# Two hybrid decoder layers on one core: attention's probabilities are turned by DMA in place of TensorE

## The chip, the core and the metric

The kernel runs on one core of a Trainium2 chip. A core has TensorE (PE; the profile lists its matrix multiplications as PE and its weight loads as PEld), VectorE (DVE), ScalarE (ACT), GpSimd (POOL) and SyncE (SP), whose queue here issues nearly all DMA transfers. The metric is the device time of one execution in microseconds, and a kernel's time is the median over its runs.

## What is computed

The reference is a trunk of two decoder layers over 256 tokens of width 1024, in float32. Each layer has a gated feed-forward network (FFN) of width 2816 added at half weight, a mixer, and a second FFN like the first:

```
for l in range(DEPTH):
    h = h + 0.5 * rmsnorm(swiglu(rmsnorm(h), ff1...))
    h = h + rmsnorm(hybrid_mixer(rmsnorm(h), ...))
    h = h + 0.5 * rmsnorm(swiglu(rmsnorm(h), ff2...))
```

The mixer projects its input and works on it with three groups side by side: a state space scan of 8 heads with a short convolution ahead of it, a pooling group, and causal attention with 4 heads of 64. For 256 tokens the attention's block choice is empty, so it is plain causal attention: `softmax(q k^T / 8)` times `v`. The three results are laid side by side and multiplied by an output matrix.

## The kernel before

Tokens lie in two tiles of 128 (t = 0, 1). Every float32 product with a weight is made of three matmuls of a shorter type: weights and inputs are split into a rounded part `hi` and a rest `lo`, and `hi*hi`, `hi*lo`, `lo*hi` are added up in PSUM.

The weights come in units of 1 MB. The class `Weights` plans them in the order of their use. `load` (line 75) issues a unit's transfer on SP into one of 4 raw buffers; `split_next` (line 95) makes `hi` on ScalarE (line 111) and `lo` on VectorE (line 112) into one of 5 pairs of buffers; `done` gives a pair back when the last matmul of the unit is in the program. `pump` (line 123) loads and splits as far as buffers allow. It loads only while `W.allowed`, a budget of loads, is above 0; `load` takes one off. If `W.behind` is set, the next load is ordered behind that transfer on SP's queue. The program text gives priorities: a scheduler lays out each engine's fixed order, taking the first instruction in the text that its model says is ready. `tc.issue_after(x)` orders instructions on one engine behind x, and `tc.keep_in_program_order` pins matmuls.

In the FFN some tiles are turned by DMA. `send` (line 482) takes a tile of 128 x 512 float32, lets ScalarE part it into its upper and lower 16-bit halves (line 485, 128 x 1024 of type uint16) and has SP issue a transposing transfer (line 489), eight blocks of 128 x 128 halves. `receive` (line 494) joins the turned halves to float32 again on ScalarE (line 497).

The mixer of one layer goes, in the order of the text: projections to q, k, v (`first`, line 712); the tap products of the convolution (`taps`, matmuls on line 327) for B, C, x0, x1; `qT`, `kT` and the scores into PSUM (line 840); `softmax` (line 843) for the first 128 queries over 128 keys (p0) and for the other 128 over 256 keys (p1), two tiles each, one for each of j = 0, 1, that hold two heads: the exponentials on ScalarE (line 854), the scaling on VectorE (line 858). Then come the segments of the scan (lines 770 and 772), three silus (line 795) and the products of B and C (lines 886 to 891). Behind these the probabilities are turned: eight transposes on PE (lines 898, 899) and four (line 905), from PSUM to `pT0` and `pT1` by three copies on ScalarE (lines 901, 908). Then taps x1, the product u for pooling (line 923, copied on line 926), the first half of z (`zed(0)`, matmuls on line 367), attention (`attend`, lines 972 and 974, which reads `pT0`, `pT1` and v), the transposes of x (line 998), the second half of z, pooling (line 1057), the scan (line 1019), its gating (lines 1027 to 1031) and turning (line 1037), and the output product (line 389, pinned). Attention and the transposes of x are ordered behind z's first half, and z's second half behind the transposes of x:

```
        sz0 = zed(0)
        d = pool_means()
        with tc.issue_after(zed.last.ins):
            y_attn = attend()
            turn_x(0)
            turn_x(1)
        with tc.issue_after(turn_x.last.ins):
            sz1 = zed(1)
```

Of the kernel before, what the change touches and what calls it, by code (L numbers as in the profile page):

```python
# [13 lines left out]
U16 = mybir.dt.uint16  # L14
AF = mybir.ActivationFunctionType
# [3 lines left out]
P = 128  # L19
# [128 lines left out]
def hybrid_trunk_kernel(ctx: ExitStack, tc: tile.TileContext, a, out: bass.AP):  # L148
    nc = tc.nc
# [9 lines left out]
    def buf(dtype=F32, n=512, tag="t"):  # L159
        return tmp.tile([P, n], dtype, tag=tag, name=f"{tag}{next(ids)}", bufs={"t": 20, "n": 8}[tag])  # L160

    def tiny(n):
        return small.tile([P, n], F32, tag=f"s{n}", name=f"s{next(ids)}", bufs=2 if n > 64 else 12)

    def bank(tag="wk"):
        return psum.tile([P, 512], F32, tag=tag, name=f"{tag}{next(ids)}")

    def banks2():
        return [bank("acc"), bank("acc")]

    W = Weights(tc, rawp, splitp)

    h = consts.tile([P, NT, D], F32, name="h")
# [6 lines left out]
    ident = consts.tile([P, P], F32, name="ident")  # L180
# [274 lines left out]
    def ffn_first(t, p, pin=False, ahead=None, between=None, by_dma=False):  # L455

        ps = [bank(), bank()]
        for i in range(2):
            mm_half(ps[i], [p["f", i, k] for k in range(2)], t, pin, ahead if i else None)
            if not i:  # L460
                s = buf()
                nc.scalar.activation(s, ps[0], AF.Silu)
        hf = gate(*ps, s)
        with tc.issue_after(pre_turn.lower.ins):
            if between:
                W.split_next()
                between()

            W.pump(SPLIT_BUFS - t)
        return send(hf) if by_dma else hf  # L470
# [8 lines left out]
                    nc.tensor.transpose(ps[:, j * S + t * P : j * S + (t + 1) * P], hf[t][:, c], ident)  # L479
            split_into(hT[i], (slice(None), slice(None)), ps)  # L480

    def send(x):

        halves = buf(U16, 1024)
        part = nc.scalar.activation(halves.rearrange("p (a n) -> p a n", a=2),
                                    x[:, :].bitcast(U16).rearrange("p (n a) -> p a n", a=2), AF.Copy)
        turned = buf(U16, 1024)
        with tc.issue_after(part.ins):
            t = nc.sync.dma_start_transpose(turned.rearrange("p (a n) -> p a n", a=8), halves)
        if W.allowed < 10:  # L490
            W.allowed, W.behind = 10**6, t.ins
        return turned

# [44 lines left out]
    def ffn_quad(i, p, left, turn, downs, by_dma):  # L538
# [41 lines left out]
        def second():  # L580
            product(pd, left["X22"], p["T4", i], False)
            nc.scalar.activation(w2, pd, AF.Silu)
            nc.vector.tensor_tensor(h1, h1, w2, op=ALU.mult)
            hf[1] = send(h1) if by_dma else h1
            W.pump()
# [121 lines left out]
    def mixer(l, p, turned, next_left, before_next):  # L707
# [42 lines left out]
        z, z2, q = tiny(16), tiny(16), tiny(16)  # L750
# [42 lines left out]
        def act(name, acc):  # L793
            conv[name] = buf()
            return nc.scalar.activation(conv[name], acc, AF.Silu)
# [6 lines left out]
        for w in range(2):  # L802
            ps = bank("acc")
# [4 lines left out]
            c = buf()  # L808
# [27 lines left out]
        for n, ps in ((P, s0), (2 * P, s1)):  # L836
            for pr in range(2):
                for j in range(2):
                    r = slice(j * 64, (j + 1) * 64)
# [2 lines left out]

        def softmax(ps, n):

            pr_ = [buf(n=2 * n) for _ in range(2)]
            mx, sm = tiny(4), tiny(4)
            for j in range(2):
                nc.vector.tensor_reduce(mx[:, 2 * j : 2 * j + 2], ps[j][:, : 2 * n].rearrange("p (a n) -> p a n", a=2),
                                        axis=AX.X, op=ALU.max)
            nc.vector.tensor_scalar(mx, mx, -0.125, None, op0=ALU.mult)  # L850
            for j in range(2):
                for a in range(2):
                    s, i = slice(a * n, (a + 1) * n), slice(2 * j + a, 2 * j + a + 1)
                    nc.scalar.activation(pr_[j][:, s], ps[j][:, s], AF.Exp, scale=0.125, bias=mx[:, i], accum_out=sm[:, i])
            nc.vector.reciprocal(sm, sm)
            for j in range(2):
                x = pr_[j].rearrange("p (a n) -> p a n", a=2)
                nc.vector.tensor_tensor(x, x, sm[:, 2 * j : 2 * j + 2, None].to_broadcast([P, 2, n]), op=ALU.mult)
            return pr_

        p0 = softmax(s0, P)
        p1 = softmax(s1, 2 * P)


        ps = bank()
# [10 lines left out]
        act("B", accB)  # L876
        act("C", accC)
        act("x0", accx)
        W.pump()


        cbs = []
        for g in range(2):
            B_, C_ = conv["B"][:, g * 256 : (g + 1) * 256], conv["C"][:, g * 256 : (g + 1) * 256]
            ps = bank("acc")
            nc.tensor.matmul(ps[:, : 2 * P], B_[:, :P], C_, start=True, stop=True)
            nc.tensor.matmul(ps[:, 2 * P : 3 * P], B_[:, P:], C_[:, P:], start=True, stop=True)
            c = buf(n=384).rearrange("p (b n) -> p b n", b=3)
            ps = ps[:, :384].rearrange("p (b n) -> p b n", b=3)
# [1 line left out]
            nc.scalar.activation(c[:, 1, :], ps[:, 1, :], AF.Copy)  # L891
            cbs.append(c)

        pT0 = [None, None]
        for j in range(2):
            ps = bank("acc")
            for pr in range(2):
                nc.tensor.transpose(ps[:, pr * 256 : pr * 256 + P], p0[j][:, pr * P : (pr + 1) * P], ident)
                nc.tensor.transpose(ps[:, pr * 256 + P : (pr + 1) * 256], p1[j][:, pr * 256 : pr * 256 + P], ident)
            pT0[j] = buf()  # L900
            nc.scalar.activation(pT0[j], ps, AF.Copy)
        ps = bank("acc")
        for j in range(2):
            for pr in range(2):
                nc.tensor.transpose(ps[:, (2 * j + pr) * P : (2 * j + pr + 1) * P],
                                    p1[j][:, pr * 256 + P : (pr + 1) * 256], ident)
        pT1 = buf()
        nc.scalar.activation(pT1, ps, AF.Copy)

        for c in range(2):  # L910
            for g in range(2):
# [12 lines left out]
        W.done(p["u"])  # L924
        u = buf()
        nc.scalar.activation(u, pu, AF.Copy)
        W.pump()

        def pool_means():
# [135 lines left out]
        acc = [banks2(), banks2()]  # L1065
# [68 lines left out]
    for l in range(DEPTH):  # L1134
        def step(n):

            def f(t):
                r = pre_scale(t)
                if t == 1:
                    load_gain(1, l + n // 3, 2 * (n % 3) + 1)  # L1140
                    if 3 * l + n + 1 < 3 * DEPTH:
                        load_gain(0, l + (n + 1) // 3, 2 * ((n + 1) % 3))
                return r
            return f

        def store(t, s):
            q = nc.scalar if t == NT - 1 and s.start else nc.sync
            q.dma_start(out[t * P : (t + 1) * P, s], h[:, t, s])

        f1, mx, f2 = plans[l]  # L1150
        end = l == DEPTH - 1
        turned = ffn(l, 1, f1, FFN_GAIN, turned, left, None, step(1), False, None if l else later)
        left = {}
        turned = mixer(l, mx, turned, left, step(2))
        left, now = None if end else {}, left
        turned = ffn(l, 2, f2, FFN_GAIN, turned, now, left, store if end else step(3), end)
# [98 lines left out]
```

## Time and profile before

| what | value |
|---|---|
| median of 3 runs | 924.17 us (924.09 to 925.56) |
| the profiled execution | 923.65 us |
| its span, first to last instruction | 922.0 us |
| granted TensorE clock, mean | 0.997 |
| ScalarE busy | 627.0 us (68%) |
| the mixer's stage in layer 0, 205 to 281 us | PE busy 76.00 of 76 us, VectorE 63.87, ScalarE 50.60 |

The profile is of one execution. Busy times are sums over an engine's instructions; a matmul's length is drawn as if it stood alone, so that neighbours overlap. A row of the timeline gives start, length, engine, line, operation, what it writes and reads, how many instructions are merged in it, and in brackets how long the engine was idle ahead of it and which instruction ended that. The two layers are alike in the mixer: layer 1 runs 449.8 us behind layer 0 at these lines.

### The profile page before, as it was taken

Reading aid. Unit: us, or ns where it says so; the run is one execution under the profiler, and the core shown is the slowest. Engines: PE = TensorE matmul, PEld = TensorE weight load, DVE = VectorE, ACT = ScalarE, POOL = GpSimd, SP = SyncE. Lnnn points to the kernel's source line nnn. Section 1 sums busy time; section 2 is a strip of 40 time slices with the busy share of each in tenths; the row PEclk is TensorE's granted clock in tenths of the full one; section 3 lists DMA queues with packets and bytes.
Section 4 is the critical chain, followed back from the end, with each engine's and each line's share of the span. In section 5 each row is a group of like instructions: output and inputs, shape, how many; then the busy total and the mean of one; then the engine's idle time right before and its main releaser. Section 6 shows DMA issues by size and latency. Waiting matters only on the chain.

```text
span 922.0 us, 12352 instructions
## 1 busy us (share of the span) xinstructions
PE 909.3 (99%) x4626; PEld 769.0 (83%) x4626; DVE 800.9 (87%) x1067; ACT 627.0 (68%) x1003; POOL 30.2 (3%) x49
## 2 busy tenths in 40 slices
PE   8999999999999999999999999999999999999997
PEld 5888887889988888888888888888998888888885
DVE  6999889689877999899599989987989699989972
ACT  7666657478747677667675866766795566867761
POOL 0000000000001000000000000000000110000000
PEclk9999999999999999999999999999999999999999
DMA  8576957556434577768655958593834145959641
GB/s 335 158 267 199 365 180 287 216 192 220 147 136 147 149 257 214 281 183 334 179 183 149 351 163 295 173 334 139 296 111 157 73 171 165 347 145 324 190 142 46
DMA packets 40671, 193.64 MB, mean 210 GB/s; under 512 B 15778, under 2 KB 16034, under 8 KB 18596
## 3 DMA queue, kind: packets, MB, share of 16 engines
q1 hardware_dynamic: 38740, 180.01, 54.2%
q0 software_dynamic: 1728, 12.58, 7.3%
q8 instruction: 36, 0.59, 0.2%
q10 hardware_dynamic: 144, 0.26, 0.1%
q14 instruction: 23, 0.19, 0.1%
HBM read 188.65 MB, written 1.05 MB: 206 GB/s over the span
## 4 chain that ended last, share of the span: by engine, by line
PE 95%; DVE 2%; issue 2%; ACT 1%; DVEq 0%; POOLq 0%; POOL 0%
PE acc L389 30%; PE wk L534 23%; PE wk L367 14%; PE wk L336 10%; PE wk L327 6%; PE wk L338 5%; DVE lo L112 1%; PE wk L354 1%; PE wk L278 1%; PE wk L1019 1%; PE wk L508 1%; PE acc L770 0%; PE acc L1102 0%; PE wk L479 0%; PE acc L840 0%
## 5 line engine op out<-in xcount | busy, mean ns | idle before, releaser
L112 DVE TENSOR_TENSOR lo<-raw,hi 128x1024 fp32r<-128x1024 f32 (+2 forms) x452 | 464.7, 1076 | 20.9 <-ACT hi L111 18.5
L111 ACT ACTIVATE hi<-raw 128x1024 fp32r<-128x1024 f32 (+2 forms) x452 | 399.8, 937 | 118.8 <-DMA raw<-in_ff_d 32.7
L389 PE MATMUL acc<-hi,t 128*128 128x512 f32 x832 | 215.9, 391 | 0.3 <-ACT t L227 0.3
L389 PEld LDWEIGHTS acc<-hi,t 128*128 128x128 f32 x832 | 154.6, 188 | 32.2 <-ACT t L227 1.2
L389 PE MATMUL acc<-lo,t 128*128 128x512 f32 x416 | 114.2, 390 | 0.0
L534 PE MATMUL wk<-hi,n 128*128 128x512 f32 x384 | 100.7, 390 | 0.8 <-DVE wk L560 0.8
L367 PE MATMUL wk<-hi,xT 128*128 128x512 f32 x384 | 99.6, 397 | 1.6 <-ACT hi L111 1.6
L336 PE MATMUL wk<-xT,hi 128*128 128x512 f32 x384 | 97.4, 394 | 0.0
L110 DVE TENSOR_TENSOR raw<-raw,raw 128x1024 f32<-128x1024 f32 x72 | 86.2, 1217 | 10.4 <-DMA raw<-in_ff_q 10.4
L389 PEld LDWEIGHTS acc<-lo,t 128*128 128x128 f32 x416 | 77.7, 188 | 16.0
L367 PEld LDWEIGHTS wk<-hi,xT 128*128 128x128 f32 x384 | 72.0, 191 | 16.9 <-ACT hi L111 1.9
L534 PEld LDWEIGHTS wk<-hi,n 128*128 128x128 f32 x384 | 71.7, 188 | 15.8 <-ACT hi L111 1.2
L336 PEld LDWEIGHTS wk<-xT,hi 128*128 128x128 f32 x384 | 69.9, 188 | 13.3
L534 PE MATMUL wk<-hi,xT 128*128 128x512 f32 x288 | 77.3, 390 | 0.9 <-DVE t L567 0.8
L534 PEld LDWEIGHTS wk<-hi,xT 128*128 128x128 f32 x288 | 53.7, 188 | 13.2 <-ACT hi L111 1.2
L338 PEld LDWEIGHTS wk<-xT,lo 128*128 128x128 f32 x384 | 52.3, 190 | 3.8
L338 PE MATMUL wk<-xT,lo 128*128 128x256 f32 x384 | 53.5, 282 | 0.0
L367 PE MATMUL wk<-lo,xT 128*128 128x512 f32 x192 | 51.5, 390 | 0.0
L534 PE MATMUL wk<-lo,n 128*128 128x512 f32 x192 | 51.3, 389 | 0.0
L327 PE MATMUL wk<-xT,hi 128*128 128x256 f32 x320 | 42.5, 283 | 0.0
L367 PEld LDWEIGHTS wk<-lo,xT 128*128 128x128 f32 x192 | 36.0, 188 | 7.7
L534 PEld LDWEIGHTS wk<-lo,n 128*128 128x128 f32 x192 | 36.0, 188 | 7.5
(186 smaller groups left out, 890.0 us busy)
## 6 DMA issues: line engine op xcount, KB each, us to landing
raw<-in_ff_q SPq DMA_DIRECT2D x48, 1024.0 KB, 6.6
raw<-in_ff_d SPq DMA_DIRECT2D x44, 1024.0 KB, 6.0
raw<-in_ff_f SPq DMA_DIRECT2D x16, 1024.0 KB, 5.5
raw<-in_ff_q POOLq DMA_DIRECT2D x12, 1024.0 KB, 7.9
raw<-in_ff_g SPq DMA_DIRECT2D x12, 1024.0 KB, 4.8
raw<-in_ff_u SPq DMA_DIRECT2D x12, 1024.0 KB, 5.2
raw<-in_w_in SPq DMA_DIRECT2D x10, 1024.0 KB, 4.8
raw<-in_w_kvz SPq DMA_DIRECT2D x8, 1024.0 KB, 6.4
```

The source lines that it names most:

```text
L110: nc.vector.tensor_tensor(raw[:, s], self.raw[x][:, s], self.raw[y][:, s], op=op)
L111: self.act = nc.scalar.activation(hi[:, s], raw[:, s], AF.Copy)
L112: nc.vector.tensor_tensor(lo[:, s], raw[:, s], hi[:, s].bitcast(F32), op=ALU.subtract)
L278: pre_turn.last = nc.tensor.transpose(ps[:, k * P : (k + 1) * P], xn[i][:, k * P : (k + 1) * P], ident)
L327: nc.tensor.matmul(ps, w[:, k, s], y[:, k, :], start=i == 0 and k == 0, stop=i == 2 and k == KD - 1)
L336: nc.tensor.matmul(ps, hi[:, k, s], both[:, :, k, :], start=k == 0, stop=k == KD - 1)
L338: nc.tensor.matmul(ps[:, S:], lo[:, k, s], xT[0][:, k, :], start=False, stop=k == KD - 1, skip_group_check=True)
L354: nc.tensor.matmul(ps, x[:, k, s], w[:, k, :], start=i == 0 and k == 0, stop=i == 2 and k == KD - 1)
L367: m = nc.tensor.matmul(ps, y[:, k, :], w[:, k, :], start=h == 0 and n == 0, stop=h == 1 and n == len(parts) - 1)
L389: m = nc.tensor.matmul(acc[b], x[:, j, s], w[:, j, b * 512 : (b + 1) * 512], start=first and j == 0 and i == 0, stop=last and j == 1 and i ...
L508: nc.tensor.transpose(ps[:, c], x[:, c], ident)
L534: nc.tensor.matmul(ps, x[:, k, :], w[:, k, :], start=first and n == 0, stop=n == len(parts) - 1, skip_group_check=not first)
```

## The change

The twelve transposes on PE and the three copies behind them go. Each layer instead sends three tiles, p0 as one tile of 512 columns and the two tiles of p1, with the FFN's `send`, behind the products of B and C in the text. Six copies on ScalarE, each of 128 x 512 halves, join what comes back into the same `pT0` and `pT1`; they stand behind the copy of u. The two halves of p0 now share one buffer. The budget of loads is set to 0 ahead of the sends, and the third send lifts it again and sets `W.behind`, so that the loads that `pump` had requested ahead of the turning are requested behind the third transfer.

```
-    def send(x):
+    def send(x, more=False):
...
-        if W.allowed < 10:
+        if W.allowed < 10 and not more:
             W.allowed, W.behind = 10**6, t.ins
         return turned
...
-            pr_ = [buf(n=2 * n) for _ in range(2)]
+            both_ = buf() if n == P else None
+            pr_ = [both_[:, j * 2 * n : (j + 1) * 2 * n] if n == P else buf(n=2 * n) for j in range(2)]
+            softmax.last = both_
...
         p0 = softmax(s0, P)
+        p0_all = softmax.last
         p1 = softmax(s1, 2 * P)
...
         act("x0", accx)
+        W.allowed = 0
         W.pump()
...
-        pT0 = [None, None]
-        for j in range(2):
-            ps = bank("acc")
-            for pr in range(2):
-                nc.tensor.transpose(ps[:, pr * 256 : pr * 256 + P], p0[j][:, pr * P : (pr + 1) * P], ident)
-                nc.tensor.transpose(ps[:, pr * 256 + P : (pr + 1) * 256], p1[j][:, pr * 256 : pr * 256 + P], ident)
-            pT0[j] = buf()
-            nc.scalar.activation(pT0[j], ps, AF.Copy)
-        ps = bank("acc")
-        for j in range(2):
-            for pr in range(2):
-                nc.tensor.transpose(ps[:, (2 * j + pr) * P : (2 * j + pr + 1) * P],
-                                    p1[j][:, pr * 256 + P : (pr + 1) * 256], ident)
-        pT1 = buf()
-        nc.scalar.activation(pT1, ps, AF.Copy)
+        sent = [send(p0_all, True), send(p1[0], True), send(p1[1])]
+
+        def take_probs():
+            q0, *q1 = (x.rearrange("p (a c n) -> p a c n", a=2, c=4) for x in sent)
+            pT0, pT1 = [buf(), buf()], buf()
+            d1 = pT1[:, :].bitcast(U16).rearrange("p (c n a) -> p a c n", a=2, c=4)
+            for j in range(2):
+                d0 = pT0[j][:, :].bitcast(U16).rearrange("p (r h n a) -> p a r h n", a=2, r=2, h=2)
+                nc.scalar.activation(d0[:, :, :, 0], q0[:, :, 2 * j : 2 * j + 2], AF.Copy)
+                q = q1[j].rearrange("p a (r h) n -> p a r h n", r=2)
+                nc.scalar.activation(d0[:, :, :, 1], q[:, :, :, 0], AF.Copy)
+                nc.scalar.activation(d1[:, :, 2 * j : 2 * j + 2], q[:, :, :, 1], AF.Copy)
+            return pT0, pT1
...
         u = buf()
         nc.scalar.activation(u, pu, AF.Copy)
+        pT0, pT1 = take_probs()
         W.pump()
```

## The prediction

> **What bounds the kernel now.** I read the page's busy times and its chain first, then PE's waits, the windows of the mixer, and last the timelines of PE, ScalarE, VectorE and SP around the lines that change.
>
> ```profile
> PE 909.3 (99%) x4626; PEld 769.0 (83%) x4626; DVE 800.9 (87%) x1067; ACT 627.0 (68%) x1003; POOL 30.2 (3%) x49
> ...
> PE 95%; DVE 2%; issue 2%; ACT 1%; DVEq 0%; POOLq 0%; POOL 0%
> ```
> ```profile
> PE wk L206 <- DVE n L200: 2.3, 1, 2.3
> ```
> ```profile
> 245.00:262.00 17.00, 17.00 (x101) 14.33 (x100) 16.70 (x31) 7.07 (x10) 0.00 (x0) 1.00 0.40 152
> ```
>
> TensorE is busy 99% of the span and 95% of the chain that ended last; the longest wait of any of its lines is 2.3 us, at the start. In the stage of the change (third fence: PE, weight loads, VectorE, ScalarE) PE is busy 17.00 of 17 us, VectorE 16.70 and ScalarE only 7.07. So what leaves PE's stream there shortens the kernel, so long as nothing that PE reads comes later than PE asks. VectorE has no room either, but the change gives it nothing. ScalarE has room.
>
> **What goes from PE.** First the rows of layer 0, then of layer 1.
>
> ```profile
> 240.16 0.27 PE L898 MATMUL acc<-ident,t 128*128 128x128 f32 x1
> ...
> 241.03 0.60 PE L905 MATMUL acc<-ident,t 128*128 128x128 f32 x4
> 241.38 0.48 PE L327 MATMUL wk<-xT,lo 128*128 128x256 f32 x2
> ```
> ```profile
> 689.97 0.27 PE L898 MATMUL acc<-ident,t 128*128 128x128 f32 x1
> ...
> 691.20 0.48 PE L327 MATMUL wk<-xT,lo 128*128 128x256 f32 x2
> ```
>
> Eight transposes on L898 and L899 and four on L905 stand in one block. PE starts them at 240.16 and the next matmul at 241.38: 1.22 us. In layer 1 it is 689.97 to 691.20: 1.23 us. A single one is drawn 0.27 long, but they overlap, and what the stream gets back is the distance between starts. Sum: 2.45 us.
>
> The Trainium skill, "TensorE: Matmul & The Clock Gate", Part 4 (PE-mode transpose), gives about 275 ns for a PE transpose inside a kernel; taken for each of 24, its estimate would be 6.6 us. The trace has the same length for one (0.27) and 0.10 from start to start, so the sum stays with 2.45.
>
> **What ScalarE loses and gets.** Copies taken away:
>
> ```profile
> L901 ACT ACTIVATE t<-acc 128x512 f32<-128x512 f32 x4 | 2.4, 600 | 0.0
> L908 ACT ACTIVATE t<-acc 128x512 f32<-128x512 f32 x2 | 1.2, 618 | 0.0
> ```
>
> That is 3.6/2 = 1.8 us a layer. What comes instead is known from the FFN, which sends tiles in the same way:
>
> ```profile
> L485 ACT ACTIVATE t<-t 128x1024 uint16<-128x1024 uint16 x12 | 12.5, 1046 | 2.4 <-DVE t L583 2.4
> L497 ACT ACTIVATE t<-t 128x1024 uint16<-128x1024 uint16 x12 | 16.4, 1370 | 0.0
> ```
>
> Three partings at 1.05 are 3.1 us. The six joins are L497 at half the width. The ratio I take from the split of the weights, below: four of 512 in 2.18 (0.55 each), two of 1024 in 2.01 (1.00 each). So 1.37 x 0.55 = 0.75, six of them 4.5 us; the bounds are 6 x 0.55 = 3.3 and, if the more broken pattern costs as much as the full one, 6 x 1.37 = 8.2. Net: 3.1 + 4.5 - 1.8 = 5.8 us more ScalarE a layer.
>
> ```profile
> 237.54 1.67 ACT L795 ACTIVATE t<-t 128x512 f32<-128x512 f32 x3
> 239.12 1.04 ACT L111 ACTIVATE hi<-raw 128x1024 fp32r<-128x1024 f32 x1
> ...
> 246.71 2.01 ACT L111 ACTIVATE hi<-raw 128x1024 fp32r<-128x1024 f32 x2 [1.83 <-PE wk L327]
> ...
> 249.14 0.57 ACT L926 ACTIVATE t<-wk 128x512 f32<-128x512 f32 x1
> 253.13 0.60 ACT L982 ACTIVATE t<-wk 128x512 f32<-128x512 f32 x1 [3.41 <-PE wk L367]
> 254.63 0.60 ACT L227 ACTIVATE t<-acc 128x512 fp32r<-128x512 f32 x1 [0.91 <-PE acc L974]
> 258.43 2.01 ACT L111 ACTIVATE hi<-raw 128x1024 fp32r<-128x1024 f32 x2 [3.20 <-PE wk L367]
> ...
> 261.65 2.18 ACT L111 ACTIVATE hi<-raw 128x512 fp32r<-128x512 f32 x4
> ```
>
> The idle time in brackets between 244.9 and 258.4 is 1.83 + 3.41 + 0.91 + 3.20 = 9.35 us: it holds the 5.8, and by 258.43 ScalarE is where it was. At the bound of 8.2 the sum is 9.5, which just fills it.
>
> **The path of the probabilities.** This is the new wait. What it must meet:
>
> ```profile
> 231.25 1.09 PE L770 MATMUL acc<-n,after_r 128*128 128x512 f32 x4
> 232.18 0.39 PE L327 MATMUL wk<-xT,hi 128*128 128x256 f32 x2
> ...
> 246.51 1.12 PE L327 MATMUL wk<-xT,lo 128*128 128x256 f32 x8
> ...
> 252.03 1.07 PE L367 MATMUL wk<-hi,xT 128*128 128x512 f32 x4
> 253.03 0.66 PE L972 MATMUL acc<-t,t 128*64 128x256 f32 x4
> ...
> 254.53 1.09 PE L998 MATMUL wk<-ident,t 128*128 128x128 f32 x8
> 255.38 1.18 PE L367 MATMUL wk<-hi,xT 128*128 128x512 f32 x4
> ```
> ```profile
> 234.72 1.28 DVE L858 TENSOR_TENSOR t<-t,s 128x512 f32<-128x512 f32 x2
> ```
> ```profile
> L489 SPq DMA_TRANSPOSE t<-t x12: 1238/1268/1607, 307.2 to 887.1; - x12
> ...
> DMA to landing us min/median/max: 3.0/3.9/6.6
> ```
>
> The last probabilities are scaled at 236.0. ScalarE then has exponentials, the silus of L795 to 239.2 and the split of L111 to 240.2 ahead of the partings in the text, so I let the three run from 240.3 to 243.4. SP issues a transfer in 1.27, so the second and third start as their partings end; landing takes 3.0 undisturbed, 3.9 in the median, 6.6 at worst: the third is there at 246.4, 247.3 or 250.0. I take 247.3.
>
> The joins stand behind the copy of u (L926). PE ends u at 247.63, after the change 1.22 earlier at 246.4; the copy ends at 247.0, or at 248.5 (249.71 - 1.22) if the split of 246.71 keeps its place ahead. Joins of 4.5 end at 251.5 or 253.0. PE reaches attention (L972) at 253.03 - 1.22 = 251.8. Behind it and free of it stand the eight transposes of L998 (254.53 to 255.38, 0.85 us) and the second half of z, whose first matmul is at 255.38 and which is as long as the first (5.5 us). The order of PE's stream is fitted to when operands come: at 231.25 and 232.18 the segments of L770 are broken by matmuls of L327 because their operands aren't all there. So a wait costs nothing if the transposes of L998 go first (cover to 252.65) or z (to 258); unfitted, it costs 0 to 1.2 a layer. I take 0.
>
> **Who stands behind the new waits.** On SP, the transfers wait for the partings, and the next loads stand behind the third by the change itself:
>
> ```profile
> 242.09 7.12 SPq L84 DMA_DIRECT2D raw<-in_ff_f  x2
> ```
> ```profile
> raw<-in_ff_f SPq DMA_DIRECT2D x16, 1024.0 KB, 5.5
> ```
>
> The first of these moves from 242.09 to about 244.7 (243.4 + 1.27) and lands 5.5 later at 250.2; its split is at 261.65. Cover: 11 us. The second starts at 248.9 (242.09 + 7.12 less an issue of 0.33) and doesn't move. Cost nothing. The held budget of loads touches only this one, since the third send lifts it before the next buffer comes free, and the tile shared by the first probabilities adds no instruction. On ScalarE, behind the joins stand the splits and silu of the rows above; the first to be missed on PE is z's silu, through the gating on VectorE:
>
> ```profile
> 262.30 2.50 DVE L112 TENSOR_TENSOR lo<-raw,hi 128x512 fp32r<-128x512 f32 x4 [0.37 <-ACT hi L111]
> 265.25 0.69 DVE L228 TENSOR_TENSOR t<-t,t 128x512 fp32r<-128x512 f32 x1 [0.45 <-ACT t L227]
> ...
> 269.14 0.75 DVE L1031 SCALAR_TENSOR_TENSOR t<-t,s,row 128x512 f32<-128x512 f32 x1 [1.87 <-POOL s L240]
> ```
> ```profile
> 271.75 0.60 PE L1037 MATMUL wk<-ident,t 128*128 128x128 f32 x4
> ```
>
> L1031 ends at 269.89 and PE reads it at 271.75: 1.86 us of slack. With PE 1.22 ahead and VectorE unmoved, 0.64 is left; the idle 0.37 and 0.45 ahead of it were waits for ScalarE that followed PE, so they go too, and 1.4 is left. VectorE may therefore come up to 1.4 us later (partings ahead of a split, say) at no cost. From there on, the pinned rows of the output product and the FFN start from PE's own matmuls, and the gain stands.
>
> **Sum.** The profiled execution took 923.65 us for its span of 922.0; the median of the runs is 924.17, 0.52 above it. 923.65 - 2.45 = 921.2; against the median 924.17 - 2.45 = 921.7.
>
> **Rivals.** (a) PE asks too early: attention stays right behind z's first half and the joins end at 253.0, with wider joins at up to 254: 1.2 to 2.2 us a layer back, 924.1 to 926.1, no change. For it: ScalarE's order is one queue. Against: PE's stream elsewhere hardly waits. Chance 0.20.
>
> (b) Slower: the transfers run one behind the other's landing. The first is issued at 241.4; three at the median of 3.9 end at 253.1, two joins of 0.75 follow: 254.6, against 251.8: 2.8 a layer, 924.17 - 2.45 + 5.6 = 927.3. At the worst landing of 6.6 it would be 261.2 + 1.5 - 251.8 = 10.9 a layer, 943.5. It decides from a wait of 2.15 a layer, (2.45 + 1.85)/2, that is when the third lands after 252.45. For it: no row of before shows two such transfers in flight. Against: 1.27 of issue is far under 3.0, and z's second half can go first. Chance 0.12. The Trainium skill speaks for this side: "VectorE: DVE Perf Modes", the three transpose paths, prices a 128x128 block at 390 ns on TensorE and 1309 by DMA and prefers TensorE where PSUM will do; its 24 blocks in a row would be 31 us by estimate. Here a transfer of eight blocks landed in 3.0 to 6.6, so the trace doesn't bear that out.
>
> (c) The removal doesn't count, because VectorE sets L1031: if its work comes over 1.4 later, the gain shrinks by the rest, to nothing at 2.6: 924.2. Chance 0.06.
>
> (d) Each transpose is worth its drawn length: 24 x 0.27 = 6.5, 917.7. The starts 0.10 apart speak against it. Chance 0.02.
>
> **Numbers.** A measurement of this kernel tells about 0.2% (1.85 us) from no change. Forecast 0.60, with its own range of 921.0 to 922.3 (waits of up to 0.3 a layer, or that much less). Faster: 0.60 + 0.02 = 0.62. Same: 0.20 + 0.06 = 0.26. Slower: 0.12. The range takes in (c), most of (a) and the near edge below the forecast: 920.8 to 925.8; outside lie (b), (d) and the end of (a).
>
> **What would show it.** Right: L898, L899 and L905 gone, the next matmuls of L327 1.2 earlier, and L1037 ahead by 1.2 in layer 0 and 2.4 in layer 1; three transfers about 1.3 apart, landing before 250; joins of about 0.75. Wrong: a PE wait at the lines of attention for a join, transfers 3 or more apart, joins over 1.2, or a wait at L1037 for VectorE.

## The result, and the profile after

The changed kernel takes 934.78 us (median of 5 runs, 932.22 to 935.62) against 924.17 before (now 5 runs, 923.77 to 925.56): a ratio of 1.0109, 95% interval 1.0095 to 1.0122. Ratios compare undisturbed runs alone and are not the quotient of the two medians, which would be 1.0115 here. The forecast was 921.7; the result is slower and lies outside the range. The profiled execution of after is the median one: 934.78 us for a span of 932.8, at a granted clock of 0.998.

The page of after, its busy times and its chain of waits:

```profile
PE 912.3 (98%) x4602; PEld 764.2 (82%) x4602; DVE 800.6 (86%) x1067; ACT 636.1 (68%) x1015; POOL 30.2 (3%) x49
...
PE 76%; DVE 13%; issue 4%; DMA 4%; ACT 2%; POOL 0%; DVEq 0%; POOLq 0%; ACTq 0%
```

TensorE has 24 matmuls fewer and is drawn busy for 3 us longer. What says more is the chain: TensorE held 95% of it before and holds 76% now, and VectorE has 13%. The path has moved to other engines.

**In which stages the time came.** I take as a mixer's length the time from the first matmul of its projections (the first row of L354) to the first product on L534 in the FFN behind it. PE's timeline of before, then of after, both layers:

```profile
192.91 1.13 PE L354 MATMUL wk<-hi,xT 128*128 128x264 f32 x8
...
313.01 1.07 PE L534 MATMUL wk<-hi,xT 128*128 128x512 f32 x4
...
642.72 1.13 PE L354 MATMUL wk<-hi,xT 128*128 128x264 f32 x8
...
762.83 1.07 PE L534 MATMUL wk<-hi,xT 128*128 128x512 f32 x4
```
```profile
192.75 1.13 PE L354 MATMUL wk<-hi,xT 128*128 128x264 f32 x8
...
316.41 1.07 PE L534 MATMUL wk<-hi,xT 128*128 128x512 f32 x4
...
648.62 1.13 PE L354 MATMUL wk<-hi,xT 128*128 128x264 f32 x8
...
772.27 1.07 PE L534 MATMUL wk<-hi,xT 128*128 128x512 f32 x4
```

The mixer takes 313.01 - 192.91 = 120.10 before and 123.66 after, and in layer 1 120.11 and 123.65. So each mixer is 3.55 us longer where the forecast has it 1.22 shorter. The FFNs between the mixers go from 329.71 to 332.21 and what is left to the span's end from 159.1 to 160.5. The sum is 7.1 + 2.5 + 1.4 - 0.2 (ahead of the first mixer) = 10.8, the difference of the spans.

**What came as forecast.** SP's queue, ScalarE's timeline and PE's, layer 0, after:

```profile
243.13 4.11 SPq L489 DMA_TRANSPOSE t<-t  x3
247.34 1.01 SPq L84 DMA_DIRECT2D raw<-in_ff_f  x2
```
```profile
242.07 1.04 ACT L485 ACTIVATE t<-t 128x1024 uint16<-128x1024 uint16 x1
...
250.99 0.78 ACT L906 ACTIVATE t<-t 128x512 uint16<-128x512 uint16 x1
...
254.11 0.75 ACT L909 ACTIVATE t<-t 128x512 uint16<-128x512 uint16 x1
```
```profile
245.02 1.12 PE L327 MATMUL wk<-xT,lo 128*128 128x256 f32 x8
```

The three transfers are issued within 4.11 us, one behind the other and not behind each other's landing. The partings take 1.04, the joins 0.75 to 0.78, and the first join starts at 250.99 without an idle time in brackets: everything had landed. Of PE's stream u's last segment stands at 245.02 in place of 246.51. Up to here the block of 1.22 us is gone (0.16 of the 1.49 lay ahead of the mixer).

**Where it is lost.** PE's timeline of after, from the transposes of x on:

```profile
251.46 1.03 PE L1001 MATMUL wk<-ident,t 128*128 128x128 f32 x8
252.45 0.65 PE L975 MATMUL acc<-t,t 128*64 128x256 f32 x2
253.03 0.50 PE L367 MATMUL wk<-hi,xT 128*128 128x512 f32 x1
253.46 0.43 PE L977 MATMUL acc<-t,t 128*64 128x128 f32 x2
253.82 0.97 PE L367 MATMUL wk<-hi,xT 128*128 128x512 f32 x3
254.72 0.65 PE L975 MATMUL acc<-t,t 128*64 128x256 f32 x2
...
261.64 1.13 PE L1060 MATMUL acc<-t,vec 128*128 128x256 f32 x4 [0.29 <-DVE t L953]
```

Attention (L975, L977), one block of 16 before, is broken up: it stands in four pieces, at 252.45, 253.46, 254.72 and 256.19, between matmuls of z's second half (L367), fitted to joins that come one at a time. VectorE's and ScalarE's timelines of after over the same time:

```profile
259.76 1.23 DVE L112 TENSOR_TENSOR lo<-raw,hi 128x1024 fp32r<-128x1024 f32 x1 [4.26 <-ACT hi L111]
260.90 0.68 DVE L953 TENSOR_TENSOR t<-t,t 128x512 f32<-128x512 f32 x1
...
275.42 0.69 DVE L1031 TENSOR_TENSOR t<-t,t 128x512 f32<-128x512 f32 x1
```
```profile
258.66 1.06 ACT L111 ACTIVATE hi<-raw 128x1024 fp32r<-128x1024 f32 x1 [3.36 <-PE wk L367]
259.63 0.58 ACT L227 ACTIVATE t<-acc 128x512 fp32r<-128x512 f32 x1
...
276.14 0.63 ACT L235 ACTIVATE n<-t 128x512 bf16<-128x512 f32 x1 [4.36 <-DVE t L1031]
...
277.10 0.36 ACT L227 ACTIVATE t<-wk 128x256 fp32r<-128x256 f32 x1
```
```profile
273.32 0.66 PE L1040 MATMUL wk<-ident,t 128*128 128x128 f32 x4 [0.23 <-DVE t L1034]
...
277.51 1.20 PE L389 MATMUL acc<-hi,t 128*128 128x512 f32 x4 [1.72 <-ACT t L227]
```

A piece of a weights' split (L111 on ScalarE, L112 on VectorE) now stands in both queues ahead of the mixer's own work. ScalarE can't do it until TensorE gives back z's first pair of buffers, and VectorE idles 4.26 us behind it, with pooling's last step (L953) and the scaling of x (L992) queued there. So the second tile's gating (L1031) starts at 275.42, and TensorE waits 1.72 us for a split at L389. Ahead of that it comes to the turning of the first tile (L1040, L1037 of before) 1.73 us late, counted from the mixer's start (80.57 for 78.84 us), nearly all of it from its own stream: the wait there is 0.23. The same place in before, on VectorE, ScalarE and PE:

```profile
272.05 0.69 DVE L1028 TENSOR_TENSOR t<-t,t 128x512 f32<-128x512 f32 x1
```
```profile
272.77 0.63 ACT L235 ACTIVATE n<-t 128x512 bf16<-128x512 f32 x1 [4.36 <-DVE t L1028]
...
273.73 0.36 ACT L227 ACTIVATE t<-wk 128x256 fp32r<-128x256 f32 x1
```
```profile
273.12 1.08 PE L389 MATMUL acc<-lo,t 128*128 128x512 f32 x4
274.15 1.20 PE L389 MATMUL acc<-hi,t 128*128 128x512 f32 x4
```

This is the row the prediction lacks. ScalarE takes the second tile's square (L235, which waits for VectorE's gating) ahead of the split of the **first** turned tile (L227), which ends at 274.09; TensorE starts the product on it at 274.15, where its own work would have let it start at about 274.03 (273.12 and four starts 0.23 apart). Here there is no slack.

### The profile page after: what moved, and what is told of

Its sections match the earlier page's. It is cut to its first block, busy times and chain, and to the rows that moved or that the text cites. A ratio compares the mean times of both kernels' runs of the same rounds, so it can differ in the third digit from the quotient of the medians.

```text
span 932.8 us, 12335 instructions
## 1 busy us (share of the span) xinstructions
PE 912.3 (98%) x4602; PEld 764.2 (82%) x4602; DVE 800.6 (86%) x1067; ACT 636.1 (68%) x1015; POOL 30.2 (3%) x49
## 4 chain that ended last, share of the span: by engine, by line
PE 76%; DVE 13%; issue 4%; DMA 4%; ACT 2%; POOL 0%; DVEq 0%; POOLq 0%; ACTq 0%
PE acc L389 22%; PE wk L534 16%; PE wk L367 13%; PE wk L336 8%; DVE lo L112 7%; PE wk L327 6%; PE wk L338 4%; DMA raw<-in_ff_q 3%; DVE raw L110 1%; PE wk L354 1%; PE wk L278 1%; ACT hi L111 1%; DMA raw<-in_ff_d 1%; DVE t L992 1%; DVE t L228 1%
## 5 line engine op out<-in xcount | busy, mean ns | idle before, releaser
L112 DVE TENSOR_TENSOR lo<-raw,hi 128x1024 fp32r<-128x1024 f32 (+2 forms) x452 | 465.1, 1075 | 31.6 <-ACT hi L111 29.0
L111 ACT ACTIVATE hi<-raw 128x1024 fp32r<-128x1024 f32 (+2 forms) x452 | 400.2, 937 | 129.5 <-DMA raw<-in_ff_d 34.0
L389 PE MATMUL acc<-hi,t 128*128 128x512 f32 x832 | 215.8, 391 | 3.7 <-ACT t L227 3.7
L389 PEld LDWEIGHTS acc<-hi,t 128*128 128x128 f32 x832 | 154.6, 188 | 35.7 <-ACT t L227 4.8
L389 PE MATMUL acc<-lo,t 128*128 128x512 f32 x416 | 114.2, 390 | 0.0
L534 PE MATMUL wk<-hi,n 128*128 128x512 f32 x384 | 100.9, 391 | 1.9 <-ACT hi L111 1.2
L367 PE MATMUL wk<-hi,xT 128*128 128x512 f32 x384 | 99.1, 394 | 1.8 <-ACT hi L111 1.8
L110 DVE TENSOR_TENSOR raw<-raw,raw 128x1024 f32<-128x1024 f32 x72 | 86.1, 1216 | 13.9 <-DMA raw<-in_ff_q 13.9
L389 PEld LDWEIGHTS acc<-lo,t 128*128 128x128 f32 x416 | 77.7, 188 | 16.0
L534 PEld LDWEIGHTS wk<-hi,n 128*128 128x128 f32 x384 | 71.6, 188 | 17.7 <-ACT hi L111 3.1
L367 PEld LDWEIGHTS wk<-hi,xT 128*128 128x128 f32 x384 | 70.9, 188 | 18.1 <-ACT hi L111 2.6
L336 PEld LDWEIGHTS wk<-xT,hi 128*128 128x128 f32 x384 | 69.9, 188 | 13.3
L534 PE MATMUL wk<-hi,xT 128*128 128x512 f32 x288 | 77.6, 391 | 2.6 <-DVE t L567 2.6
L534 PEld LDWEIGHTS wk<-hi,xT 128*128 128x128 f32 x288 | 53.6, 188 | 15.7 <-ACT hi L111 2.6
L367 PE MATMUL wk<-lo,xT 128*128 128x512 f32 x192 | 53.1, 395 | 0.1
L534 PE MATMUL wk<-lo,n 128*128 128x512 f32 x192 | 51.4, 389 | 0.0
L367 PEld LDWEIGHTS wk<-lo,xT 128*128 128x128 f32 x192 | 35.7, 188 | 9.8 <-DVE lo L112 1.6
L534 PEld LDWEIGHTS wk<-lo,n 128*128 128x128 f32 x192 | 36.0, 188 | 7.6
```

The lines of the kernel that those rows point to most:

```text
L110: nc.vector.tensor_tensor(raw[:, s], self.raw[x][:, s], self.raw[y][:, s], op=op)
L111: self.act = nc.scalar.activation(hi[:, s], raw[:, s], AF.Copy)
L112: nc.vector.tensor_tensor(lo[:, s], raw[:, s], hi[:, s].bitcast(F32), op=ALU.subtract)
L336: nc.tensor.matmul(ps, hi[:, k, s], both[:, :, k, :], start=k == 0, stop=k == KD - 1)
L367: m = nc.tensor.matmul(ps, y[:, k, :], w[:, k, :], start=h == 0 and n == 0, stop=h == 1 and n == len(parts) - 1)
L389: m = nc.tensor.matmul(acc[b], x[:, j, s], w[:, j, b * 512 : (b + 1) * 512], start=first and j == 0 and i == 0, stop=last and j == 1 and i ...
```

## The experiments

The theory after this comparison, **V**: the mixer ends when VectorE's gating of the second tile lets it, one for one, because of ScalarE's order; and what made VectorE late is the new order of the queues (**O**: a split ahead of the mixer's own work, attention broken up). Rivals: the hold of the loads costs (**H**); the DMA turn itself does, by late probabilities or ScalarE's 5.8 us; the 1.22 us were never worth anything.

All runs but the last three follow, with the ratio to the kernel before. That kernel was measured again beside each group of runs, so two kernels with nearly the same median can have different ratios. "Gating" is the start of the second tile's gating product (L1028 of before) less the start of the mixer's first L354, in layer 0.

| kernel | median us | ratio, 95% | mixer | gating | mixer - gating |
|---|---|---|---|---|---|
| before | 924.17 | | 120.10 | 79.14 | 40.96 |
| after | 934.78 | 1.0109 (1.0095-1.0122) | 123.66 | 82.67 | 40.99 |
| e1_order | 931.05 | 1.0074 (1.0059-1.0089) | 121.88 | 80.91 | 40.97 |
| e3_nohold | 938.18 | 1.0150 (1.0135-1.0166) | 125.62 | 84.67 | 40.95 |
| e7_between | 930.04 | 1.0067 (1.0049-1.0085) | 121.57 | 80.60 | 40.97 |
| e4_noturn | 925.17 | 1.0013 (0.9999-1.0026) | 119.10 | 78.13 | 40.97 |
| e11_dose | 927.77 | 1.0040 (1.0026-1.0054) | 121.54 | 80.57 | 40.97 |
| e9_copy_first | 926.04 | 1.0013 (1.0000-1.0026) | 119.46 | 78.46 | 41.00 |
| e6_attn_late | 932.10 | 1.0074 (1.0060-1.0089) | 122.04 | 81.08 | 40.96 |
| e14_hold_only | 925.68 | 1.0006 (0.9997-1.0015) | 120.10 | 79.11 | 40.99 |
| e13_before_again | 925.35 | 1.0005 (0.9993-1.0017) | 120.11 | 79.12 | 40.99 |
| e10_turn_first | 929.84 | 1.0050 (1.0032-1.0069) | 121.66 | 83.02 | 38.64 |
| e12_all | 924.47 | 1.0000 (0.9989-1.0010) | 118.58 | 79.87 | 38.71 |
| e16_late_turn_first | 933.18 | 1.0086 (1.0062-1.0111) | 121.42 | 81.08 | 40.34 |

The last column is V: over a range of 6.5 us the mixer follows the gating within 0.05, in every kernel that keeps ScalarE's order, and only in the three that change it (below the rest) does it not.

**Is there slack? e11_dose:** work added to VectorE in the kernel before.

```
         d = pool_means()
+        dose = buf()
+        for _ in range(4):
+            nc.vector.tensor_tensor(dose, cnt, cnt, op=ALU.add)
```

> The kernel before, with four more VectorE additions of 128x512 (about 0.6 us each, so 2.4 us a layer) behind the pooling's means; nobody reads what they give. Theory S (the prediction's slack: VectorE may come 1.86 us later at the weight-by-row product without cost, and it idles 0.8 us on the way): at most 0.3 us a layer, so 924.2 to 924.8 and mixers of 120.1 to 120.4 us. Theory V (the mixer has no slack against VectorE, because ScalarE takes the second tile's square, which waits for VectorE's gating, ahead of the split of the first turned tile, for which TensorE waits): 1.6 to 2.4 us a layer, mixers of 121.7 to 122.5 us, 927.4 to 929.0. The gating product of the second tile ends as much later as the mixer grows.

Measured: mixers of 121.54 and 121.60, 1.0040, 927.77 us. VectorE's row of the gating and TensorE's of the product:

```profile
272.83 0.69 DVE L1028 TENSOR_TENSOR t<-t,t 128x512 f32<-128x512 f32 x1
```
```profile
274.93 1.20 PE L389 MATMUL acc<-hi,t 128*128 128x512 f32 x4 [1.37 <-ACT t L227]
```

This mixer starts at 192.26, so the gating is 1.43 us late and the mixer 1.44 longer (V had expected at least 1.6); of the 2.4 us added, the idle time of about 0.8 took some. For the end of the mixer the slack of 1.86 us doesn't exist.

**e10_turn_first:** after, with the second tile's gating behind the first turned split.

```
-            yn1 = gated(1, y1, sz1)
...
         gated_turn(0, yn0)
+        with tc.issue_after(gated_turn.first.ins):
+            yn1 = gated(1, y1, sz1)
```

> The changed kernel, with the second tile's square, norm and gating product placed on ScalarE and VectorE behind the first split of the first turned tile. VectorE's chain comes as late as in the changed kernel. Theory V (ScalarE's place for that square is what turns VectorE's lateness into time): TensorE's wait of 1.7 us ahead of the product with the weights' first rows goes, mixers of 121.9 to 122.2 us in place of 123.66, and the time falls by 3.0 to 3.6 us against the changed kernel's 934.8, to 931.2 to 931.8. If the product's own start was what was late (VectorE's split of the first tile, or the weights), the wait stays and the mixers stay at 123.5 or more.

Measured: mixers of 121.66 and 121.63, 929.84 us. ScalarE and PE:

```profile
274.44 0.39 ACT L227 ACTIVATE t<-wk 128x256 fp32r<-128x256 f32 x1 [2.22 <-PE wk L1040]
...
276.91 0.63 ACT L235 ACTIVATE n<-t 128x512 bf16<-128x512 f32 x1 [1.14 <-DVE t L1031]
```
```profile
276.07 1.07 PE L389 MATMUL acc<-hi,t 128*128 128x512 f32 x4
```

The split comes first, the row at 276.07 has no wait, and each mixer is 2.0 us shorter, though VectorE's gating is as late as in after. Theory V is shown from both sides. The time falls by 4.9 where 3.0 to 3.6 were expected. The Trainium skill, "Perfetto Trace Analysis", Tensor Engine Instruction, says that ScalarE and VectorE work strictly first in, first out; the trace agrees: in after L227 starts at 277.10, behind a square that waited 4.36 us.

**What made VectorE late? e1_order:** after, with the splits of the second z's pump placed behind attention's copy (ScalarE) and the scaling of x (VectorE).

```
+            with ExitStack() as order:
+                for x in (split_into.last, by_head.last):
+                    order.enter_context(tc.issue_after(x.ins))
+                W.pump()
```

> The change, with one order added: the weights split during z's second half (on ScalarE behind the copy of attention's result, on VectorE behind the scaling of x) can't come ahead of pooling's last step and the scaling of x. Loads stay held. Theory O (order): in the changed kernel VectorE waits 4.26 us a layer at a split whose buffer PE gives back only in z's second half, with pooling and the scaling of x behind it; the mixers then end late and the FFNs behind them lose more. Here about 2 us of that wait stay, since attention's split comes first and attention ends late: 926 to 929. Theory S (stream): PE loses about 2.0 a layer because attention's matmuls are broken into those of z; alone it predicts no change from 934.8. Theory H (hold): the loads requested late starve what follows; no change from 934.8.

```profile
257.54 0.69 DVE L228 TENSOR_TENSOR t<-acc,t 128x512 fp32r<-128x512 f32 x1 [2.49 <-ACT t L227]
```

Measured: mixers of 121.88, 931.05 us. Half of the mixer's loss is gone; the time misses the 926 to 929 of theory O. What is left is that VectorE waits 2.49 us for attention, which is still broken up and late.

**e3_nohold:** after without `W.allowed = 0`.

> The change without the hold: the budget of loads is not set to 0, so that loads are requested as before the change; the sends and joins stay. VectorE's order comes out as before the change (pooling and the scaling of x ahead of the split). Theory O: like the run with the order mended, 926 to 929. Theory H: what the FFNs lose (3.8 us over three of them) and whatever of the mixer came from late loads returns, more than in the run with the order mended. Theory S alone: attention is still broken into z, 933 to 935.

```profile
262.36 0.69 DVE L228 TENSOR_TENSOR t<-acc,t 128x512 fp32r<-128x512 f32 x1 [4.37 <-ACT t L227]
```

A miss: the slowest of all, mixers of 125.62 and 938.18 us. The third transfer goes out behind a load on SP, at 248.62, the joins come late, and VectorE waits 4.37 us for attention's split. VectorE's own order is that of before, as expected, but on ScalarE a weights' split (259.84 to 261.85) still stands ahead of attention's copy, which starts at 261.75 although attention is done by 259.3. So in this kernel the hold helps. **e14_hold_only** puts the hold alone into the kernel before (`W.allowed = 0` ahead of the block of transposes, lifted behind it).

> The kernel before with only the hold of the loads: the budget is set to 0 where the changed kernel does it and lifted again in the text behind the twelve transposes, so nothing is turned by DMA. Theory V: the order of VectorE's operations ahead of the gating stays that of before, so the mixers stay at 120.0 to 120.4 us and the time at 924 to 926. If holding the loads is what costs (weights late for their splits), the mixers grow by over 1 us and the time by over 2.5.

Measured: mixers of 120.10, 1.0006. The hold alone costs nothing, and e3 is slower without it; H is false.

**e7_between:** after, with attention unbroken between the two halves of z's second product, behind the scaling of x, and the splits behind that scaling.

```
+            if mid and h == 1:
+                with tc.issue_after(m.ins):
+                    behind = mid()
...
-            y_attn = attend()
...
-            sz1 = zed(1)
+            sz1 = zed(1, lambda: (by_head.last,), mid)
+        y_attn = held[0]
```

> The change, loads held, with attention in one piece between the two halves of z's second product, and with pooling's last step and the scaling of x ahead of the next split on VectorE. Theories O and S together: PE gets back 2.0 a layer, VectorE's 4.3 go, the FFNs lose nothing: 921 to 923, faster than before the change. O alone: 926 or better, but with PE's loss left. H: 930 or more, since the loads are held as in the change.

```profile
259.90 2.19 ACT L111 ACTIVATE hi<-raw 128x512 fp32r<-128x512 f32 x4 [2.44 <-PE wk L374]
262.00 0.57 ACT L227 ACTIVATE t<-acc 128x512 fp32r<-128x512 f32 x1
```

A miss: 930.04, mixers of 121.57. Now another unit's split, waiting for TensorE, stands on ScalarE ahead of attention's copy, and VectorE waits 2.06 us for it. **e9_copy_first** puts that split behind the copy too:

```
-                W.pump()
+                copied, scaled = behind()
+                with tc.issue_after(scaled.ins):
+                    W.split_next()
+                    with tc.issue_after(copied.ins):
+                        W.pump()
```

> The changed kernel with attention's products unbroken between the two halves of z's second product, and with the weights' splits behind attention's copy on ScalarE and behind the scaling of x on VectorE. Theory V with O (the whole loss is that weight splits stand ahead of the mixer's own work in the fixed orders of ScalarE and VectorE, and that attention's products are broken up): VectorE's gating of the second tile is back at about 271.5 to 272 us, mixers of 119.2 to 119.9 us against 120.1 before, time 922.5 to 924.5. If the DMA turn costs something of itself (ScalarE's partings and joins or the late loads), the mixers stay above 121 us and the time above 926.

```profile
273.31 1.21 PE L396 MATMUL acc<-hi,t 128*128 128x512 f32 x4 [0.55 <-ACT t L227]
```

The mixers are as expected, 119.46 and 119.41: 0.65 below before, with the DMA turn, its partings and joins all in it. V still holds here: the row shows TensorE waiting 0.55 us for the split. Without any turn the mixer takes 119.10 (e4, below), so with attention moved behind the joins the turn itself costs at most 0.36 us; the rest of the loss is O. The time, 926.04, is not as expected: 1.0013 where the mixers alone give 922.9. The rest of this section comes back to that.

**e6_attn_late** tries the simplest mend, one line moved: attention behind all of z.

```
-            y_attn = attend()
             turn_x(0)
             turn_x(1)
         with tc.issue_after(turn_x.last.ins):
             sz1 = zed(1)
         with tc.issue_after(zed.last.ins):
+            y_attn = attend()
```

> The changed kernel with one line moved: attention's products stand in the text behind the whole of z, not behind its first half, so they come unbroken, the scaling of x comes ahead of the weights' splits on VectorE, and the splits don't wait for a buffer that attention has delayed. Theory V: VectorE's gating of the second tile is back at about 272 us, mixers of 119.4 to 120.4 us (attention's own split, now late, may hold the output product's first matmuls by a few tenths), time 924 to 927 with what has been lost outside the mixers in the other kernels. If late probabilities or ScalarE's extra work were the cost, the mixers stay above 121.5 and the time above 928.

```profile
255.15 2.01 ACT L111 ACTIVATE hi<-raw 128x1024 fp32r<-128x1024 f32 x2
```
```profile
256.25 1.23 DVE L112 TENSOR_TENSOR lo<-raw,hi 128x1024 fp32r<-128x1024 f32 x1 [3.15 <-ACT hi L111]
```
```profile
261.14 1.13 PE L1060 MATMUL acc<-t,vec 128*128 128x256 f32 x4 [1.80 <-DVE t L953]
```

A miss: mixers of 122.04, 932.10 us. A split has got ahead again, this time of pooling's steps, and TensorE waits 1.80 us for them. The numbers are those expected if ScalarE's extra work costs (above 121.5 and 928), and here it does: ScalarE had no idle time ahead of that split, which stood behind the joins. Its new work costs where VectorE's next step waits for a split behind the joins; e9 shows that this need not be so. **e16_late_turn_first** adds the edit of e10 to it.

> The last kernel with the second tile's square behind the first turned split on ScalarE as well. Theory V: mixers of 118.6 to 119.6 us, time 922 to 926; it is the candidate to beat both kernels, which it does only if the stages outside the mixers lose less than 2 us.

Also a miss: mixers of 121.42, 933.18 us.

**Can the gain be had? e4_noturn:** before without the twelve transposes; ScalarE copies the probabilities unturned, so attention's product is another one. It shows what the removal alone is worth.

```
-                nc.tensor.transpose(ps[:, pr * 256 : pr * 256 + P], p0[j][:, pr * P : (pr + 1) * P], ident)
...
-            nc.scalar.activation(pT0[j], ps, AF.Copy)
+            nc.scalar.activation(pT0[j][:, :256], p0[j], AF.Copy)
+            nc.scalar.activation(pT0[j][:, 256:], p1[j][:, :256], AF.Copy)
```

> The kernel before with the twelve transposes left out: ScalarE copies the unturned probabilities from SBUF, so attention's product is another one. It has no transfers, joins or held loads. If the block on PE is worth the 1.22 us a layer that stand between its first start and the next matmul: 921.7. If VectorE sets the pace of the mixer and the removal is worth nothing: 924.2.

Measured: each mixer 1.0 us shorter, and the time 1.0013 times before (0.9999 to 1.0026): no gain. **e12_all** is e9 and e10 together, the best mend found.

> The edits of the last two together: attention unbroken, splits behind the mixer's own work, and the second tile's square behind the first turned split. Theory V: mixers of 118.4 to 119.0 us, time 921 to 923, so 1 to 3 us below the kernel before. If the gains of the two do not add (the same 1.7 us), mixers of 119.2 to 119.9 and 922.5 to 924.5.

The mixers, 118.58, are 1.52 us shorter than before, as expected; the time, 924.47 (ratio 1.0000, 0.9989 to 1.0010), is not: no better than before. No kernel of this study beats before by the 0.2% that a measurement can tell.

**What the stages outside the mixers do. e13_before_again** is the kernel before, unchanged.

> The kernel before once more, as if it were a change: it gives a second profile of it and says what a comparison gives when nothing is changed. Expected: ratio 1.000 within 0.0015, mixers of 120.1 us as in its first profile (they have agreed within 0.05 us between the layers in every kernel). If the stages outside the mixers vary between executions, as the 922.3 to 927.4 us of its runs suggest, they come out 1 to 3 us longer here than the 488.8 us of its first profile (which at 923.65 was one of its faster executions). If they come out at 488.8 again, the 2 to 4 us that all the changed kernels lose outside the mixers is caused by the edits.

The mixers agree to 0.06 us, yet the FFNs between them take 331.18 us where the first profile has 329.71 (644.43 - 313.25). The rows of PE's waits, after and e13_before_again; in the first profile of before the same lines wait 0.8 + 0.8 us:

```profile
PE wk L534 <- DVE t L567: 2.6, 4, 1.1
...
PE wk L534 <- ACT hi L111: 1.2, 2, 1.0
PE wk L534 <- DVE wk L560: 0.8, 1, 0.8
```
```profile
PE wk L534 <- DVE t L567: 1.5, 4, 0.5
PE wk L534 <- ACT hi L111: 0.6, 1, 0.6
PE wk L534 <- DVE wk L560: 0.5, 1, 0.5
```

So one execution can differ from another there: the span less two mixers is 681.7 us in the first profile of before, 683.6 in e13 and 685.5 in after. But that isn't all: the median less two mixers is 684.0 to 685.5 us in every kernel that keeps the twelve transposes (before, e11, e13, e14, e17), and 686.5 to 690.3 in every kernel without them, e4 too. It is a matter of medians: e4's profiled execution, its fastest at 921.65, has 681.8 us there, as before. A guess was that the transposes advance the ring of four accumulator banks in PSUM, so that the FFNs add up in other banks. **e17_one_bank** adds one unused bank a layer to before; **e18_all_banks** and **e19_noturn_banks** add three to e12 and e4:

```
+        for _ in range(3):
+            nc.vector.memset(bank("acc")[:, :1], 0.0)
```

> The kernel before with one accumulator bank more per layer, in which VectorE writes one column and which nobody reads: the ring of four banks then stands at the mixer's end where it stands in the changed kernel (one on is three back). Theory B (which physical banks the FFNs accumulate in costs the 2 us outside the mixers): about 2 us over the kernel before, ratio 1.0015 to 1.003. If the banks don't matter: ratio 1.000 within 0.0012. Mixers 120.1 to 120.3 in both.

> The mended kernel (attention unbroken, splits behind the mixer's work, the square behind the turned split) with three accumulator banks more per layer, each written in one column, so that the ring stands as in the kernel before. Theory B: about 2 us off its 0.0% against the kernel before, so 0.2% faster than that kernel, ratio 0.9975 to 0.9985. If the banks don't matter: ratio 0.999 to 1.001 as without them.

> The kernel before without the twelve transposes (ScalarE copies the unturned probabilities, so attention's product is another one), with three accumulator banks more per layer, so that the ring stands as in the kernel before. Theory B: 2 us off its 1.0013, ratio 0.9985 to 0.9995. If the banks don't matter: 1.000 to 1.0025 again.

Measured: 0.9985 (0.9975 to 0.9996), 1.0000 (0.9984 to 1.0015) and 0.9994 (0.9981 to 1.0006). The ratio of e19 alone is one that theory B expected, though its median is that of e4 (925.18 and 925.17), from which only the banks differ. But e17, with the banks of the changed kernel, should have been slower and is not, and e18 gains nothing. So the banks don't do it.

The traces show where it goes, though not why. In the FFN behind layer 1's mixer TensorE, ScalarE and VectorE run the same instructions in the same order in all 17 kernels. From the first product on L534 to the end it takes 159.1 to 159.3 us in the five that keep the transposes and 159.4 to 162.3 in the other twelve. ScalarE waits there for weight units to land (the transfers of line 84) 9.7 to 12.5 us in the five and 13.3 to 18.0 in the twelve. In after, for example, VectorE waits 5.0 us at one of its sums of weights (L110) where in before it waits 2.7, and TensorE then waits 1.1 us for VectorE at L534. So weights that land late for their splits go with the loss; why they do stays open.

## Why the prediction was wrong

- **The removal** of the block: right. TensorE has the 1.22 us in its stream (u at 245.02 for 246.51), and without the transposes a mixer is 1.0 shorter (e4).
- **ScalarE's durations and the transfers:** right. Partings 1.04, joins 0.75, transfers issued about 1.4 apart. The probabilities' time was not: the joins are done at 254.9 and not at 251.5 to 253.0, because the copy of u ahead of them started only at 250.51, behind a silu that waits for VectorE. (The partings too start 1.8 later than taken, 242.07 for 240.3, and the first load behind the transfers goes out at 247.34, not 244.7.) Rivals (b) and (d) are out.
- **"So a wait costs nothing if the transposes of L998 go first ... or z ...; unfitted, it costs 0 to 1.2 a layer. I take 0":** wrong. PE's order was fitted to the joins, and the fitting cost. From the transposes of x to pooling it takes 10.2 us in after, 0.29 of it a wait, and 8.06 with attention in one piece (the last section); the same matmuls take 7.9 in before (253.03 to 260.95). That is part of rival (a), which had the joins late but not attention broken up.
- **Who stands behind ScalarE:** the prediction counted its idle time (9.35 us) against the new work (5.8) and concluded that nothing moves. It didn't ask whether the orders of the queues stay. They didn't: a split moved ahead of the mixer's work on ScalarE and VectorE, and VectorE's idle time went from 0.8 to over 4.
- **"With PE 1.22 ahead and VectorE unmoved": this is the step that failed.** VectorE's work was put at no change, because the edit gives it nothing to do. Its gating comes 3.53 us late (82.67 for 79.14 from the mixer's start), from the new orders. By the prediction's own slack of 1.86 that would have made a mixer 1.7 us longer in place of 1.22 shorter.
- **"VectorE may therefore come up to 1.4 us later ... at no cost" failed with it,** and makes the rest, 1.9 a mixer. The 1.86 us were read at L1037, the first tile's way. The second tile's gating has no reader on TensorE so early; but ScalarE, in order, holds the first tile's split behind it. With that row read, the slack is 0, and a late VectorE costs one for one (e11).
- **Rival (c)** had the mechanism, VectorE setting the end, and was bounded wrongly: "the gain shrinks by the rest, to nothing at 2.6". It was held to be a loss of the gain, with a slack in front of it that isn't there. A VectorE 3.53 us late makes the mixer 3.55 longer.
- **Outside the mixers** the prediction had nothing change; there the transposes' absence goes with 2 us, whose cause is not found.

## What to carry to other kernels

Slack is read at every engine that takes operands in a fixed order, not only where the late result's own reader stands: look for what is queued behind the instruction that waits for it. And when an edit shifts when operands are due, price the orders that the scheduler will lay out anew; a wait that moves ahead of another engine's work can cost more than all that the edit removes. A dose of idle work on an engine (e11) tells in one run whether its slack is real.

## What the runs showed of the hardware

Attention's matmuls take TensorE less time in one block than in pieces. PE's timeline of e12_all, where attention (lines 982 and 984) is one block:

```profile
252.13 1.03 PE L1015 MATMUL wk<-ident,t 128*128 128x128 f32 x8
...
255.83 0.66 PE L982 MATMUL acc<-t,t 128*64 128x256 f32 x4
...
257.33 1.19 PE L374 MATMUL wk<-hi,xT 128*128 128x512 f32 x4
...
260.19 1.02 PE L1084 MATMUL acc<-t,vec 128*128 128x256 f32 x4
```

The same matmuls, from the transposes of x to pooling, take 8.06 us here and 10.18 - 0.29 = 9.89 in after, 1.83 more. Over half of it lies within attention. The trace lists a head's float32 product as two matmuls. In the block two heads, which write the two halves of the output's rows, go side by side, with starts 0.01 to 0.06 us apart: L982's four matmuls in the row above take 0.66 us. In after the joins come one by one, each of the first three pieces is one head's product alone, and two matmuls of L975 take 0.65. The block holds TensorE for 1.50 us (255.83 to 257.33), the four pieces for 0.58 + 0.36 + 0.57 + 1.01 = 2.52 (each from its start to the next matmul of z).

The other 0.8 goes with six more changes between attention's matmuls and others; short waits that show as no idle time may be in it. The Trainium skill, "TensorEngine Tiling (Array Packing)", Key Properties, says that changing the tiling mode drains TensorE; attention's matmuls load 64 columns (128*64) and z's 128, and the trace agrees: in the block of e12_all attention's first matmul starts 0.32 us behind z's last, where z's own follow each other by 0.23.
